# The MLP up product of a one-core encoder block, half of its K-tiles taken as seven quarter products

## The chip, the cores and the metric

The kernel runs on one core of a Trainium2 chip. The metric is the device time of one execution in microseconds, the median of three runs. The engines are named as the profile names them: PE is TensorE (PEld its weight loads), DVE VectorE, ACT ScalarE, POOL GpSimd, SP SyncE, whose queue issues nearly all DMAs here.

## The reference

One layer of an encoder for 256 tokens of width 2,048, all in float32. Only the last product group (the MLP) is touched in its arithmetic:

```python
    for l in range(DEPTH):                       # DEPTH = 1
        xn = rmsnorm(h, norm_mix_w[l])
        proj = xn @ w_in[l]                      # 2,048 x 14,352
        ...                                      # gated linear attention, spatial gating, gates
        h = h + mixed @ w_out[l]
        hn = rmsnorm(h, norm_mlp_w[l])
        h = h + jnp.square(jax.nn.relu(hn @ w_ff_up[l])) @ w_ff_down[l]   # 2,048 x 8,192 and back
    return rmsnorm(h, norm_final_w)
```

## The kernel before, in words

The 256 tokens are two halves (`tt` = 0, 1) of 128. Every large product runs in `gemm`: for one block of 512 output columns it walks the 16 K-tiles of 128 rows in eight pairs. For each pair it loads a 128 x 1,024 block of weights (512 KB, tile `w`), and `split_weights` makes two tiles of it: `wh`, the weights rounded to fp32r (a cast on ACT, line 183), and `wl`, the rest (a subtraction on DVE, line 184). Activations lie transposed as such a pair too (an `Operand`: `hi` and `lo`, in tiles of the pool `slots`, 4 K-tiles each). A product is then three matmuls of 128 x 128 by 128 x 512 into one PSUM bank: hi by `wh`, lo by `wh`, hi by `wl` (lines 201 to 203). So one pair of weight tiles serves 2 K-tiles x 2 halves x 3 = 12 matmuls. There are five `w` buffers and four each of `wh` and `wl`, so ACT casts into a buffer that PE gave back three pieces before the piece is needed.

A finished column block is evicted, and what is to be done with it later (transposes by DVE and a round trip through a DRAM tile `scratch`, in `to_operand_vector`; transposes by PE in `to_operand`) is put on the list `pending`; `gemm` takes one entry off it for each pair of K-tiles (`drain`). Below this code a list scheduler sets each engine's order; semaphores and buffers are set by it too.

The MLP runs in four stages of 2,048 features: `up(st, j)` makes one of the four column blocks of the hidden layer (ACT evicts with relu and the norm's factor, line 353; DVE squares, line 764), and alternates with `down(st - 1, j)`, which multiplies the stage before by its rows of `w_ff_down` and adds the result to `h` on DVE (line 779). PSUM is two pools of four banks: `mm` for the products, `tr` for the rest.

Of the kernel before, what the change touches and what calls it, by code (L numbers as in the profile page):

```python
# [37 lines left out]


W_ROW = 1024  # L40

V_MLP, V_GLA, V_BA, V_BS = 0, 16, 20, 28
NVEC = 36
# [15 lines left out]
def block_kernel(  # L59
# [75 lines left out]
            pending.popleft()()  # L135


    h = cpool.tile([P, NTT, D], F32, name="h")
    xv = x[0].rearrange("(t p) d -> p t d", p=P)

    def load_x(b):
        s = cols(b, 2 * P)
        nc.sync.dma_start(h[:, :, s], xv[:, :, s])

    def late(dst, src):

# [27 lines left out]
    def split_weights(src, by_k=False):  # L174

        k, n = src.shape[1], src.shape[1] * src.shape[2]
        w = wpool.tile([P, W_ROW], F32, tag="w", name=uid("w"), bufs=5)
        hi = wpool.tile([P, W_ROW], F32R, tag="wh", name=uid("wh"), bufs=4)
        lo = wpool.tile([P, W_ROW], F32R, tag="wl", name=uid("wl"), bufs=4)
        wv, hv, lv = [t[:, 0:n].rearrange("p (k n) -> p k n", k=k) for t in (w, hi, lo)]  # L180
        for s in [slice(i, i + 1) for i in range(k)] if by_k else [slice(0, k)]:
            nc.sync.dma_start(wv[:, s], src[:, s])  # L182
            pin(nc.scalar.copy(hv[:, s], wv[:, s]))  # L183
            pin(nc.vector.tensor_tensor(  # L184
                lv[:, s], wv[:, s], hv[:, s].bitcast(F32), op=ALU.subtract
            ))
        return hv, lv

    def gemm(a, w, c0, n=CB, parts=1, k0=0, after=None, split_tail=False):

        ps = [[mm_ps() for _ in range(NTT)] for _ in range(parts)]
        m = n // parts
        held = []

        def products(kt, tt, hi, lo):
            ah, al = a.at(kt, tt)
            for i in range(parts):
                o = ps[i][tt][:, 0:m]
                wh = hi[kt % 2][:, cols(i, m)]
                wl = lo[kt % 2][:, cols(i, m)]  # L200
                pin(nc.tensor.matmul(o, lhsT=ah, rhs=wh, start=kt == 0, stop=False))  # L201
                pin(nc.tensor.matmul(o, lhsT=al, rhs=wh, start=False, stop=False))  # L202
                pin(nc.tensor.matmul(o, lhsT=ah, rhs=wl, start=False, stop=kt == KT - 1))  # L203

        for kb in range(KT // 2):
# [12 lines left out]
            if kb > 1 or kb == 1 and len(pending) > 6:  # L218
                drain()
            while a.ready < 2 * kb + 2:  # L220
                drain()
            if split_tail and kb >= KT // 2 - 3:
# [12 lines left out]
    def to_operand_pair(dst, src, scale=None):  # L235
# [11 lines left out]
        hi, lo = dst.hi[-1], dst.lo[-1]  # L247
        if scale is None:
# [15 lines left out]
        dst.ready += 2  # L264

    def to_operand(dst, src, scale=None):

        for half in range(2):
            part = [src[:, tt, cols(half, 2 * P)] for tt in range(NTT)]
            pending.append(lambda part=part: to_operand_pair(dst, part, scale))  # L270

    def transpose_quadrants(dst, src, jm):

# [2 lines left out]
        for i in range(4):  # L276
            nc.vector.transpose(dv[cols(jm, 32), i], sv[cols(i, 32), jm])  # L277

    def to_operand_vector(dst, src, scale=None):


        tr = []
# [14 lines left out]
        def split():  # L297
            kt0 = dst.ready
            hi, lo = slot(F32R), slot(F32R)
            dst.hi.append(hi)  # L300
            dst.lo.append(lo)

            v = flat(tr[1]).rearrange("p (m a b) -> p a m b", m=4, b=32)

            def by_quadrant(t):
                return t.rearrange("p k (t m b) -> p (k t) m b", t=NTT, b=32)

            if scale is None:
                nc.scalar.copy(by_quadrant(hi), v)  # L309
                nc.vector.tensor_tensor(  # L310
                    by_quadrant(lo), v, by_quadrant(hi).bitcast(F32), op=ALU.subtract
                )
            else:
                for k in range(4):
                    a = slice(NTT * k, NTT * (k + 1))
                    nc.scalar.activation(  # L316
                        by_quadrant(tr[0])[:, a], v[:, a], AF.Copy, scale=scale(kt0 + k)
                    )
                nc.scalar.copy(hi, tr[0])
                nc.vector.tensor_tensor(lo, tr[0], hi.bitcast(F32), op=ALU.subtract)  # L320
            dst.ready += 4

        pending.append(transpose)
# [35 lines left out]
    xsq = [cpool.tile([P, 4], F32, name=f"xsq{tt}") for tt in range(NTT)]  # L359

    def x_step(kb):
        to_operand_pair(xT, [h[:, tt, cols(kb, 2 * P)] for tt in range(NTT)], mix_col)

    def x_next(kb):
        if kb < KT // 2 - 1:
            load_x(kb + 1)
        for i in range(kb - 1, kb + kb // (KT // 2 - 1)):
            if i >= 0:
                b, tt = divmod(i, 2)
                sum_squares(xsq[tt][:, b : b + 1], h[:, tt, cols(b)])  # L370
        if kb < KT // 2 - 1:
            x_step(kb + 1)

# [372 lines left out]


    hT = Operand()
    hsq = [cpool.tile([P, 4], F32, name=f"hsq{tt}") for tt in range(NTT)]
    for j in range(4):  # L750
        ps = gemm(mT, w_out[0], j * CB)[0]
        part = h[:, :, cols(j)]
        for tt in range(NTT):
            nc.vector.tensor_tensor(part[:, tt], ps[tt], part[:, tt], op=ALU.add)
        (to_operand_vector if j < 3 else to_operand)(hT, part, lambda kt: vcol(V_MLP + kt))
# [11 lines left out]
    n_st = D_FF // D  # L767
    fsq = [cpool.tile([P, 4], F32, name=f"fsq{tt}") for tt in range(NTT)]
    wf = []

# [2 lines left out]

    def down(st, j, f):
        last = st == n_st - 1
        ps = gemm(f, w_ff_down[0], j * CB, k0=st * D, split_tail=last and j == 3)[0]
        for tt in range(NTT):
            part = h[:, tt, cols(j)]
# [20 lines left out]
    def finish(tt, m3):  # L799
# [3 lines left out]
        nc.gpsimd.tensor_tensor(r, m, mhalf[:, 0:1], op=ALU.pow)  # L803
        for j in range(4):
            t = ev_tile()
            part = h[:, tt, cols(j)]
            if j == 0:
                nc.vector.tensor_scalar_mul(t, part, r)
            elif j < 3:
# [57 lines left out]
```

## Time and profile before

| | |
|---|---|
| median of three runs | 1631.16 us |
| shortest of them | 1631.15 us |
| the profiled execution's own time | 1629.94 us |
| its span in the profile | 1627.8 us |
| PE busy | 1607.5 us (99%) |
| DVE busy | 958.6 us (59%) |
| ACT busy | 764.7 us (47%) |
| mean DMA rate | 211 GB/s |

The span is the stretch that the profiler saw; the execution's own time is 2.1 us longer, and the median of the runs lies 1.2 us above that. Matmuls are pipelined, so a row of 0.39 us of PE does not mean that PE took 0.39 us for it: how fast it works is read from the starts of rows that follow each other.

### The profile page before, as it was taken

How to read it: one execution, taken by the hardware profiler on the slowest of the kernel's cores; microseconds unless marked ns; L12 is line 12 of the kernel's file. 1: busy time of each engine (PE TensorE's matmuls, PEld its weight loads, DVE VectorE, ACT ScalarE, POOL GpSimd, SP SyncE). 2: the span in 40 equal slices, each digit the busy share in tenths (PEclk: the TensorE clock that was granted, in tenths of full speed). 3: DMA queues.
4: the chain of work that ended last, by engine and by line, in shares of the span. 5: the costliest groups of instructions: out<-in, count | busy, mean ns of one | idle time of the engine just before them, and what ended most of it. 6: DMA issues, size and time to landing. Idle time of an engine off the chain costs nothing.

```text
span 1627.8 us, 19169 instructions
## 1 busy us (share of the span) xinstructions
PE 1607.5 (99%) x7224; PEld 1331.3 (82%) x7224; DVE 958.6 (59%) x1053; ACT 764.7 (47%) x879; POOL 23.3 (1%) x50
## 2 busy tenths in 40 slices
PE   8999999999999999999999999999999999999997
PEld 6877888888888888888888888888888888888886
DVE  5759555555555667766655656555555555555554
ACT  6475455454444444444445544444444444444443
POOL 0000000000000000000000000000000000000000
PEclk9999999999999999999999999999999999999999
DMA  7565666766666767677757777766666666767753
GB/s 242 162 200 170 180 203 202 240 207 200 200 213 184 217 209 213 219 227 225 227 186 242 219 225 241 245 220 219 219 218 213 207 214 214 223 218 220 243 194 113
DMA packets 184821, 343.20 MB, mean 211 GB/s; under 512 B 12340, under 2 KB 31080, under 8 KB 184728
## 3 DMA queue, kind: packets, MB, share of 16 engines
q1 hardware_dynamic: 181744, 337.82, 66.7%
q10 hardware_dynamic: 2984, 4.16, 0.8%
q8 instruction: 56, 0.92, 0.2%
q14 instruction: 37, 0.30, 0.1%
HBM read 324.10 MB, written 17.83 MB: 210 GB/s over the span
## 4 chain that ended last, share of the span: by engine, by line
PE 97%; DVE 1%; issue 0%; ACT 0%; DMA 0%; SPq 0%; POOL 0%; ACTq 0%; POOLq 0%; DVEq 0%
PE mm L201 32%; PE mm L203 32%; PE mm L202 32%; DVE slot L277 1%; PE tr L588 1%; DVE wl L184 1%; PE tr L636 1%; PE tr L731 0%; DMA h<-in_x_dram 0%; PE tr L245 0%; ACT wh L183 0%; PE tr L491 0%; POOL col L333 0%; SPq L182 0%; PE tr L439 0%
## 5 line engine op out<-in xcount | busy, mean ns | idle before, releaser
L184 DVE TENSOR_TENSOR wl<-w,wh 128x1024 fp32r<-128x1024 f32 (+2 forms) x585 | 704.4, 1206 | 611.0 <-ACT wh L183 594.5
L183 ACT CAST wh<-w 128x1024 fp32r<-128x1024 f32 (+2 forms) x585 | 608.0, 1040 | 779.4 <-PE mm L202 758.4
L201 PE MATMUL mm<-wh,slot 128*128 128x512 f32 (+1 forms) x2336 | 905.6, 388 | 2.2 <-ACT pair L468 2.2
L203 PE MATMUL mm<-wl,slot 128*128 128x512 f32 (+1 forms) x2336 | 903.5, 387 | 2.3 <-DVE wl L184 2.3
L202 PE MATMUL mm<-wh,slot 128*128 128x512 f32 (+1 forms) x2336 | 903.1, 387 | 0.0
L203 PEld LDWEIGHTS mm<-wl,slot 128*128 128x128 f32 x2336 | 438.9, 188 | 93.7 <-DVE wl L184 4.5
L201 PEld LDWEIGHTS mm<-wh,slot 128*128 128x128 f32 x2336 | 439.1, 188 | 90.7 <-ACT pair L468 2.4
L202 PEld LDWEIGHTS mm<-wh,slot 128*128 128x128 f32 x2336 | 439.1, 188 | 88.0
L353 ACT ACTIVATE pair<-mm,rstd 128x512 f32<-128x512 f32 x58 | 39.5, 688 | 28.5 <-PE mm L203 28.3
L289 DVE STREAM_TRANSPOSE slot<-pair 128x512 f32<-128x512 f32 x54 | 36.1, 696 | 0.8
L333 POOL TENSOR_TENSOR col<-col,mhalf 128x1 f32<-128x1 f32 (+1 forms) x20 | 17.9, 895 | 863.9 <-DVE col L331 575.8
L310 DVE TENSOR_TENSOR slot<-slot,slot 128x1024 fp32r<-128x1024 f32 x23 | 28.0, 1218 | 2.1 <-ACT slot L309 2.1
L277 DVE STREAM_TRANSPOSE slot<-pair 32x256 f32<-32x256 f32 x64 | 27.9, 436 | 1.0
L779 DVE TENSOR_TENSOR h<-mm,h 128x512 f32<-128x512 f32 x32 | 22.0, 692 | 6.8 <-PE mm L203 6.8
L309 ACT CAST slot<-slot 128x1024 fp32r<-128x1024 f32 x23 | 24.1, 1048 | 0.0
L764 DVE TENSOR_TENSOR pair<-pair 128x1024 f32<-128x1024 f32 x16 | 19.5, 1219 | 0.0
L339 ACT ACTIVATE ev<-h 128x512 f32<-128x512 f32 x24 | 15.0, 626 | 7.9 <-DVE h L779 7.9
L260 DVE SCALAR_TENSOR_TENSOR slot<-tr,mixw,slot 128x256 fp32r<-128x256 f32 x16 | 7.0, 480 | 11.5 <-ACT slot L255 11.5
L316 ACT ACTIVATE slot<-slot,vec 128x256 f32<-128x256 f32 x28 | 11.9, 498 | 0.0
L255 ACT ACTIVATE slot<-tr,mixw 128x256 fp32r<-128x256 f32 x16 | 6.7, 471 | 10.6 <-PE tr L245 10.6
L671 DVE SCALAR_TENSOR_TENSOR pair<-mm,rstd,bg 128x512 f32<-128x512 f32 x16 | 11.4, 750 | 0.0
L718 DVE TENSOR_TENSOR pair<-pair,slot 128x512 f32<-128x512 f32 x16 | 11.0, 685 | 0.1
(103 smaller groups left out, 269.5 us busy)
## 6 DMA issues: line engine op xcount, KB each, us to landing
w<-in_w_in_dram SPq DMA_DIRECT2D x215, 512.0 KB, 3.8
w<-in_w_ff_up_dram SPq DMA_DIRECT2D x128, 512.0 KB, 3.8
w<-in_w_ff_down_dram SPq DMA_DIRECT2D x128, 512.0 KB, 3.5
w<-in_w_branch_dram SPq DMA_DIRECT2D x64, 512.0 KB, 4.1
w<-in_w_out_dram SPq DMA_DIRECT2D x32, 512.0 KB, 4.8
scratch<-slot SPq DMA_DIRECT2D x120, 128.0 KB, 2.7
slot<-scratch SPq DMA_DIRECT2D x30, 512.0 KB, 5.6
w<-in_w_in_dram SPq DMA_DIRECT2D x16, 264.0 KB, 2.7
```

The source lines that it names most:

```text
L183: pin(nc.scalar.copy(hv[:, s], wv[:, s]))
L184: pin(nc.vector.tensor_tensor(lv[:, s], wv[:, s], hv[:, s].bitcast(F32), op=ALU.subtract))
L201: pin(nc.tensor.matmul(o, lhsT=ah, rhs=wh, start=kt == 0, stop=False))
L202: pin(nc.tensor.matmul(o, lhsT=al, rhs=wh, start=False, stop=False))
L203: pin(nc.tensor.matmul(o, lhsT=ah, rhs=wl, start=False, stop=kt == KT - 1))
L277: nc.vector.transpose(dv[cols(jm, 32), i], sv[cols(i, 32), jm])
L289: nc.vector.transpose(blocks[:, tt], sv[:, tt])
L309: nc.scalar.copy(by_quadrant(hi), v)
L310: nc.vector.tensor_tensor(by_quadrant(lo), v, by_quadrant(hi).bitcast(F32), op=ALU.subtract)
L353: nc.scalar.activation(res[:, tt, :], ps[tt], func, scale=scale[tt])
L764: nc.vector.tensor_tensor(a, a, a, op=ALU.mult)
L779: nc.vector.tensor_tensor(part, ps[tt], part, op=ALU.add)
```

## The change

The hidden layer is now made in eight stages of 1,024 features (two column blocks), each made whole before the `down` products of the stage before it. The first stage is still made by `gemm`. While it runs, the entries of `prepare` come off `pending`, two at a time: they scale the transposed activations by the norm's factor (`row_scale`, `norm`), and build the left factors of the scheme, seven quarters or sums and differences of quarters of 128 tokens x 512 of K, each split in hi and lo.

The seven other stages are made by `pair_gemm`. Of the 16 K-tiles, the first 8 go by Strassen's scheme (in Winograd's form): the tokens are halved, the 1,024 rows of K are halved, the 1,024 columns are halved, and in place of eight products of quarters there are seven, named "1" to "7". The right factors are four weight blocks and sums of them, made on DVE in fp32 for two K-tiles at a time: one sum in a tile `s`, three in place in the `w` tiles (`b01`, `b00`, `b10`). A factor is split as before, and serves 6 matmuls (2 K-tiles x 3). The other 8 K-tiles are done plainly (`plain`, 12 matmuls for each split). The seven results lie in all eight PSUM banks together with the plain ones, and are joined by DVE after the last product (lines 939 to 955). One pair of column blocks has thus 7 x 12 + 96 = 180 matmuls, where `gemm` has 192.

Beside this: eight `w` buffers in place of five; `h` lies in four tiles of the pool `slots`, is given up after its norm and loaded again from `x` for the residual; `x` is loaded two blocks ahead; the second part of the one product that is computed in two parts (`parts=2`) has its banks from `tr`; the squares are made on ACT; the `down` products walk 8 K-tiles for each block, so that they are added to `h` twice as often.

```diff
+W_BUFS = 8
...
-    h = cpool.tile([P, NTT, D], F32, name="h")
+    h = [pair_tile() for _ in range(4)]
...
-        w = wpool.tile([P, W_ROW], F32, tag="w", name=uid("w"), bufs=5)
+        w = wpool.tile([P, W_ROW], F32, tag="w", name=uid("w"), bufs=W_BUFS)
...
-    def gemm(a, w, c0, n=CB, parts=1, k0=0, after=None, split_tail=False):
-
-        ps = [[mm_ps() for _ in range(NTT)] for _ in range(parts)]
+    def gemm(a, w, c0, n=CB, parts=1, k0=0, nk=KT, after=None, split_tail=False, jobs=1):
+
+        ps = [[(tr_ps if i else mm_ps)() for _ in range(NTT)] for i in range(parts)]
...
     def x_next(kb):
-        if kb < KT // 2 - 1:
-            load_x(kb + 1)
+        for b in (1, 2) if kb == 0 else (kb + 2,):
+            if b < KT // 2:
+                load_x(b)
...
+    h = []
     for j in range(4):
+        part = pair_tile()
+        h.append(part)
+        late(part, xv[:, :, cols(j)])
         ps = gemm(mT, w_out[0], j * CB)[0]
...
-    def up(st, j, f):
-        ps = gemm(hT, w_ff_up[0], st * D + j * CB)[0]
-        a = scaled(ps, rstd2, AF.Relu)
-        nc.vector.tensor_tensor(a, a, a, op=ALU.mult)
-        to_operand_vector(f, a)
...
+    def row_scale(dst, rstds):
+
+        tp = tr_ps()
+        for tt in range(NTT):
+            wide = ev_tile()[:, 0:P]
+            nc.scalar.activation(wide, ident, AF.Identity, scale=0.0, bias=rstds[tt])
+            nc.tensor.matmul(tp[:, cols(tt, P)], lhsT=wide, rhs=ident, start=True, stop=True)
+        nc.vector.tensor_copy(dst, tp[:, 0:T])
...
+        steps = [lambda: row_scale(row, rstds)]
+        steps += [lambda b=b: norm(b) for b in range(2)]
+        steps.append(lambda: (plain("1", 0, 0), plain("2", 0, 1)))
+        steps.append(lambda: difference("5", 0, (1, 0), (1, 1), sub))
+        steps.append(lambda: difference("6", 1, 0, (0, 0), sub))
+        steps.append(lambda: difference("3", 0, 1, (0, 1), add))
+        steps.append(lambda: difference("7", 1, (0, 0), (1, 0), sub))
+        steps.append(lambda: plain("4", 1, 1))
+        steps += [lambda b=b: (norm(b), rest(b)) for b in (2, 3)]
...
+    def pair_gemm(a, w, c):
+
+        bank = {n: mm_ps() for n in "243N"}
+        bank.update({n: tr_ps() for n in "1567"})
...
+        def product(name, k, src):
+            hi, lo = split(src)
+            ah, al = a.left[name]
+            for kk in range(2):
+                x, y = ah[:, k + kk, :], al[:, k + kk, :]
+                accumulate(
+                    name, ((x, hi[:, kk]), (y, hi[:, kk]), (x, lo[:, kk])),
+                    name in "1567" and k + kk == SK - 1,
+                )
...
+        order = [(kt, block) for kt in range(0, KT - 2 * SK, 2) for block in range(2)]
+        order = order[:5] + [order[6], order[5], order[7]]
+        rest = iter(order)
+        for k in range(0, SK, 2):
+            b00, b10, b11, b01 = (
+                fetch(kh * SK + k, nh) for kh, nh in ((0, 0), (1, 0), (1, 1), (0, 1))
+            )
+            s1 = weights("s", F32, 1)
+            add(s1, b00, b01)
+            add(b01, b01, b11)
+            product("1", k, b00)
+            product("2", k, b10)
+            plain(*next(rest))
+            product("3", k, b11)
+            product("5", k, s1)
+            add(b00, b00, b01)
+            plain(*next(rest))
+            product("7", k, b01)
+            product("6", k, b00)
+            add(b10, b10, b00)
+            if k == 0:
+                plain(*next(rest))
+            product("4", k, b10)
...
+            for a in pair_gemm(hM, w_ff_up[0], (c0, c0 + CB)):
+                nc.scalar.activation(a, a, AF.Relu)
+                nc.scalar.activation(a, a, AF.Square)
+                to_operand_vector(f, a)
...
-    prev = None
-    for st in range(n_st + 1):
-        f = Operand()
+    prev = hidden(0)
+    for st in range(1, n_st + 1):
+        f = hidden(st) if st < n_st else None
...
         for j in range(4):
-            if st < n_st:
-                up(st, j, f)
-            if prev is not None:
-                down(st - 1, j, prev)
+            down(st - 1, j, prev)
```

The scheduler's result can be read from the built programs. PE has 7,008 matmuls of the kind of lines 201 to 203 before and 6,924 after, of which 1,260 are those of the seven pairs. On DVE, in the middle of one `down` block before, nearly every row is a split (line 184), each for 12 matmuls; `slot` is an operand's part and `mm` a PSUM bank:

```order
L184 TENSOR_TENSOR wl_1572_8241<-w_1570_8239,wh_1571_8240 128x1024
L184 TENSOR_TENSOR wl_1577_8263<-w_1575_8261,wh_1576_8262 128x1024
L184 TENSOR_TENSOR wl_1580_8281<-w_1578_8279,wh_1579_8280 128x1024
L310 TENSOR_TENSOR slot_1569_8224<-slot_1554_8142,slot_1568_8223 128x1024
L184 TENSOR_TENSOR wl_1583_8299<-w_1581_8297,wh_1582_8298 128x1024
L779 TENSOR_TENSOR h_78<-mm_1542_8097,h_78 128x512
L779 TENSOR_TENSOR h_78<-mm_1543_8098,h_78 128x512
L184 TENSOR_TENSOR wl_1586_8317<-w_1584_8315,wh_1585_8316 128x1024
```

After, on DVE, in the middle of one pair, from the split for product "6" of the first half (`wl_1793`) to the split for the fourth plain piece (`wl_1810`); `s_1803` is the sum for product "5" of the second half, and `w_1802` its block `b01`:

```order
L871 TENSOR_TENSOR wl_1793_9130<-w_1771_9031,wh_1792_9129 128x1024
L902 TENSOR_TENSOR s_1803_9176<-w_1799_9168,w_1802_9174 128x1024
L871 TENSOR_TENSOR wl_1796_9143<-w_1794_9140,wh_1795_9142 128x1024
L902 TENSOR_TENSOR w_1802_9174<-w_1802_9174,w_1801_9172 128x1024
L871 TENSOR_TENSOR wl_1798_9159<-w_1772_9033,wh_1797_9158 128x1024
L871 TENSOR_TENSOR wl_1805_9180<-w_1799_9168,wh_1804_9179 128x1024
L871 TENSOR_TENSOR wl_1807_9190<-w_1800_9170,wh_1806_9189 128x1024
L902 TENSOR_TENSOR w_1799_9168<-w_1799_9168,w_1802_9174 128x1024
L902 TENSOR_TENSOR w_1800_9170<-w_1800_9170,w_1799_9168 128x1024
L871 TENSOR_TENSOR wl_1810_9202<-w_1808_9199,wh_1809_9201 128x1024
```

Four sums stand between the splits now; the first of them needs the last of the four blocks.

On SP, where the loads are issued in order, one `up` block before stands among the stores and the reload of `scratch` like this:

```order
L182 DMA w_1575_8261<-in_w_ff_up_dram 128x2x512
L294 DMA scratch_1555_8145<-slot_1553_8141 32x4x256 x4
L182 DMA w_1578_8279<-in_w_ff_up_dram 128x2x512
L182 DMA w_1581_8297<-in_w_ff_up_dram 128x2x512
L295 DMA slot_1554_8142<-scratch_1555_8145 128x1024
L182 DMA w_1584_8315<-in_w_ff_up_dram 128x2x512
```

Here each load is for one split. After, the loads for the second half of the same pair (`w_1799` to `w_1802` are its blocks `b00`, `b10`, `b11`, `b01`; `w_1787`, `w_1794` and `w_1808` are plain pieces):

```order
L146 DMA w_1787_9101<-in_w_ff_up_dram 128x2x512
L146 DMA w_1794_9140<-in_w_ff_up_dram 128x2x512
L146 DMA w_1799_9168<-in_w_ff_up_dram 128x2x512
L146 DMA w_1800_9170<-in_w_ff_up_dram 128x2x512
L146 DMA w_1801_9172<-in_w_ff_up_dram 128x2x512
L146 DMA w_1802_9174<-in_w_ff_up_dram 128x2x512
L146 DMA w_1808_9199<-in_w_ff_up_dram 128x2x512
```

The block `b01` is the last of the four; its load waits until DVE has done the split of the second plain piece (`wl_1789`, made of `w_1787`), which gives its buffer back.

## Rows read from the trace of the kernel before

**Rows 1.** The page: span, busy time, granted clock in 40 slices, last chain by engine.

```profile
span 1627.8 us, 19169 instructions
...
PE 1607.5 (99%) x7224; PEld 1331.3 (82%) x7224; DVE 958.6 (59%) x1053; ACT 764.7 (47%) x879; POOL 23.3 (1%) x50
...
PEclk9999999999999999999999999999999999999999
...
PE 97%; DVE 1%; issue 0%; ACT 0%; DMA 0%; SPq 0%; POOL 0%; ACTq 0%; POOLq 0%; DVEq 0%
```

**Rows 2.** Groups by line, 1000 to 1600 us: busy, mean ns | idle before.

```profile
L184 DVE TENSOR_TENSOR wl<-w,wh 128x1024 fp32r<-128x1024 f32 x221 | 270.1, 1223 | 260.1 <-ACT wh L183 249.7 <-DMA w<-in_w_ff_up_dram 10.5
L183 ACT CAST wh<-w 128x1024 fp32r<-128x1024 f32 x221 | 232.9, 1054 | 320.2 <-PE mm L202 316.9 <-PE mm L203 1.9 <-ACT ev L339 1.4
L779 DVE TENSOR_TENSOR h<-mm,h 128x512 f32<-128x512 f32 x30 | 20.6, 692 | 1.5 <-PE mm L203 1.5
...
L310 DVE TENSOR_TENSOR slot<-slot,slot 128x1024 fp32r<-128x1024 f32 x14 | 17.1, 1218 | 0.0
L289 DVE STREAM_TRANSPOSE slot<-pair 128x512 f32<-128x512 f32 x26 | 17.0, 691 | 0.4
L764 DVE TENSOR_TENSOR pair<-pair 128x1024 f32<-128x1024 f32 x13 | 15.8, 1219 | 0.0
```

**Rows 3.** Timeline of PE: start, length; twelve matmuls lie between the line-203 rows.

```profile
1201.97 0.39 PE L203 MATMUL mm<-wl,slot 128*128 128x512 f32 x1
...
1202.20 0.39 PE L201 MATMUL mm<-wh,slot 128*128 128x512 f32 x1
...
1204.69 0.39 PE L203 MATMUL mm<-wl,slot 128*128 128x512 f32 x1
```

**Rows 4.** Waits, whole span: total us, times, longest.

```profile
PEld mm L203 <- DVE wl L184: 4.5, 6, 2.0
...
PE tr L245 <- DMA h<-in_x_dram: 2.7, 1, 2.7
...
PE mm L201 <- ACT pair L468: 2.2, 1, 2.2
```

**Rows 5.** The last chain, 880 to 1000 us: four PE transposes of 128 x 128.

```profile
926.67 0.44 PE tr L245 x4
```

**Rows 6.** Timeline of DVE, 1210 to 1260 us.

```profile
1226.20 1.37 DVE L779 TENSOR_TENSOR h<-mm,h 128x512 f32<-128x512 f32 x2
...
1230.45 1.22 DVE L184 TENSOR_TENSOR wl<-w,wh 128x1024 fp32r<-128x1024 f32 x1 [1.50 <-ACT wh L183]
...
1250.76 1.22 DVE L764 TENSOR_TENSOR pair<-pair 128x1024 f32<-128x1024 f32 x1
1252.01 1.31 DVE L289 STREAM_TRANSPOSE slot<-pair 128x512 f32<-128x512 f32 x2
```

**Rows 7.** Timeline of DVE, 118 to 135 us, where its rows follow each other closely.

```profile
130.34 1.22 DVE L184 TENSOR_TENSOR wl<-w,wh 128x1024 fp32r<-128x1024 f32 x1
131.47 1.22 DVE L556 TENSOR_TENSOR slot<-slot,slot 128x1024 f32<-128x1024 f32 x1
132.61 2.35 DVE L184 TENSOR_TENSOR wl<-w,wh 128x1024 fp32r<-128x1024 f32 x2
```

**Rows 8.** DMA issues, 1000 to 1600 us: KB each, median us from issue to landing.

```profile
w<-in_w_ff_up_dram SPq DMA_DIRECT2D x92, 512.0 KB, 3.8
...
slot<-scratch SPq DMA_DIRECT2D x13, 512.0 KB, 5.6
```

**Rows 9.** The tile `w`, 1000 to 1600 us: landing of all its loads.

```profile
DMA to landing us min/median/max: 3.4/3.7/8.8
```

**Rows 10.** The last chain, 0 to 30 us: the first matmuls, and one later.

```profile
9.04 0.43 PE mm L201
...
12.88 0.40 PE mm L201
...
20.58 0.24 PE mm L201
```

**Rows 11.** Windows: us, busy by engine, granted clock, DMA share, GB/s.

```profile
1100.00:1600.00 500.00, 500.00 (x2208) 414.01 (x2207) 280.54 (x257) 218.47 (x226) 0.00 (x0) 1.00 0.68 217
1600.00:1628.00 28.00, 18.52 (x82) 15.01 (x80) 9.38 (x16) 7.66 (x12) 1.09 (x2) 0.87 0.23 75
```

More of the change, by code (lines that the diff above doesn't have):

```diff
@@ L181, in split_weights @@
         for s in [slice(i, i + 1) for i in range(k)] if by_k else [slice(0, k)]:
-            nc.sync.dma_start(wv[:, s], src[:, s])
+            load(wv[:, s], src[:, s])
             pin(nc.scalar.copy(hv[:, s], wv[:, s]))
@@ L202, in products @@
                 pin(nc.tensor.matmul(o, lhsT=al, rhs=wh, start=False, stop=False))
-                pin(nc.tensor.matmul(o, lhsT=ah, rhs=wl, start=False, stop=kt == KT - 1))
-        for kb in range(KT // 2):
+                pin(nc.tensor.matmul(o, lhsT=ah, rhs=wl, start=False, stop=kt == nk - 1))
+        for kb in range(nk // 2):
             r0 = k0 + kb * 2 * P
@@ L218, in gemm @@
             if kb > 1 or kb == 1 and len(pending) > 6:
-                drain()
+                drain(jobs)
             while a.ready < 2 * kb + 2:
                 drain()
-            if split_tail and kb >= KT // 2 - 3:
+            if split_tail and kb >= nk // 2 - 3:
                 held.append((kb, hi, lo))
@@ L320, in split @@
                 nc.vector.tensor_tensor(lo, tr[0], hi.bitcast(F32), op=ALU.subtract)
+                if keep is not None:
+                    keep.append(tr[0])
             dst.ready += 4
@@ L758, in block_kernel, with __init__ @@
     rstd2 = [row_rstd(hsq[tt], f"rstd2{tt}") for tt in range(NTT)]
-    def up(st, j, f):
-        ps = gemm(hT, w_ff_up[0], st * D + j * CB)[0]
-        a = scaled(ps, rstd2, AF.Relu)
-        nc.vector.tensor_tensor(a, a, a, op=ALU.mult)
-        to_operand_vector(f, a)
-    n_st = D_FF // D
+    SK = 4
+    class Mixed:
+        def __init__(self):
+            self.left = {}
+            self.rest = Operand()
+    def row_scale(dst, rstds):
[5 more added lines that the diff above has]
+        nc.vector.tensor_copy(dst, tp[:, 0:T])
@@ new lines, in normed, with norm, rest, quarter @@
+    def normed(src, rstds):
+        m = Mixed()
+        row = ev_tile()[:, 0:T]
+        def norm(b):
+            nc.vector.tensor_tensor(
+                src[b], src[b], row.unsqueeze(1).broadcast_to([P, 4, T]), op=ALU.mult
+            )
+        def rest(b):
+            hi, lo = slot(F32R), slot(F32R)
+            m.rest.hi.append(hi)
+            m.rest.lo.append(lo)
+            nc.scalar.copy(hi, src[b])
+            nc.vector.tensor_tensor(lo, src[b], hi.bitcast(F32), op=ALU.subtract)
+            m.rest.ready += 4
+        def quarter(i, j):
+            return src[j][:, :, cols(i, P)]
+        room, temp = [], []
+        def split_left(name, v):
+            if not room:
+                room.extend(
+                    tuple(t.rearrange("p k (s t) -> p s k t", s=2)[:, i] for t in pair)
+                    for pair in [(slot(F32R), slot(F32R))] for i in range(2)
+                )
+            hi, lo = room.pop(0)
+            nc.scalar.copy(hi, v)
+            nc.vector.tensor_tensor(lo, v, hi.bitcast(F32), op=ALU.subtract)
+            m.left[name] = hi, lo
+        def plain(name, i, j):
+            split_left(name, quarter(i, j))
+        def difference(name, i, a, b, op):
+            if not temp:
+                t = slot().rearrange("p k (s t) -> p s k t", s=2)
+                temp.extend(t[:, k] for k in range(2))
+            get = lambda v: temp[v] if isinstance(v, int) else quarter(*v)
+            nc.vector.tensor_tensor(temp[i], get(a), get(b), op=op)
+            split_left(name, temp[i])
+        sub, add = ALU.subtract, ALU.add
+        steps = [lambda: row_scale(row, rstds)]
[7 more added lines that the diff above has]
+        steps += [lambda b=b: (norm(b), rest(b)) for b in (2, 3)]
+        return m, steps
@@ new lines, in weights, with split, accumulate, fetch @@
+    def weights(tag, dt, bufs):
+        t = wpool.tile([P, W_ROW], dt, tag=tag, name=uid(tag), bufs=bufs)
+        return t.rearrange("p (k n) -> p k n", k=2)
+    def pair_gemm(a, w, c):
+        bank = {n: mm_ps() for n in "243N"}
+        bank.update({n: tr_ps() for n in "1567"})
+        begun = set()
+        def split(src):
+            hi, lo = weights("wh", F32R, 4), weights("wl", F32R, 4)
+            nc.scalar.copy(hi, src)
+            nc.vector.tensor_tensor(lo, src, hi.bitcast(F32), op=ALU.subtract)
+            return hi, lo
+        def accumulate(name, terms, last):
+            for n, (x, y) in enumerate(terms):
+                nc.tensor.matmul(
+                    bank[name], lhsT=x, rhs=y, start=name not in begun,
+                    stop=last and n == len(terms) - 1,
+                )
+                begun.add(name)
+        def product(name, k, src):
+            hi, lo = split(src)
+            ah, al = a.left[name]
+            for kk in range(2):
+                x, y = ah[:, k + kk, :], al[:, k + kk, :]
+                accumulate(
+                    name, ((x, hi[:, kk]), (y, hi[:, kk]), (x, lo[:, kk])),
+                    name in "1567" and k + kk == SK - 1,
+                )
+        def fetch(row, block):
+            t = weights("w", F32, W_BUFS)
+            load(
+                t, w[row * P : (row + 2) * P, c[block] : c[block] + CB].rearrange(
+                    "(k p) n -> p k n", p=P
+                ),
+            )
+            return t
+        def add(dst, x, y):
+            nc.vector.tensor_tensor(dst, x, y, op=ALU.add)
+        def plain(kt0, block):
+            hi, lo = split(fetch(2 * SK + kt0, block))
+            drain()
+            for kk in range(2):
+                for tt in range(NTT):
+                    x, y = a.rest.at(kt0 + kk, tt)
+                    accumulate(
+                        ("24", "3N")[block][tt], ((x, hi[:, kk]), (y, hi[:, kk]), (x, lo[:, kk])),
+                        kt0 + kk == KT - 2 * SK - 1,
+                    )
+        order = [(kt, block) for kt in range(0, KT - 2 * SK, 2) for block in range(2)]
[4 more added lines that the diff above has]
+                fetch(kh * SK + k, nh) for kh, nh in ((0, 0), (1, 0), (1, 1), (0, 1))
+            )
+            s1 = weights("s", F32, 1)
[11 more added lines that the diff above has]
+            add(b10, b10, b00)
+            if k == 0:
+                plain(*next(rest))
+            product("4", k, b10)
+        p1, u2, u3, v, z = (ev_tile() for _ in range(5))
+        nc.scalar.copy(p1, bank["1"])
+        add(u2, bank["6"], p1)
+        add(u3, bank["7"], u2)
+        nc.vector.tensor_tensor(v, bank["5"], u2, op=ALU.subtract)
+        nc.vector.tensor_tensor(z, bank["5"], u3, op=ALU.subtract)
+        res = [pair_tile() for _ in range(2)]
+        left = list(rest)
+        for n, (kt, block) in enumerate(left):
+            plain(kt, block)
+            if all(b != block for _, b in left[n + 1 :]):
+                for tt in range(NTT):
+                    add(
+                        res[block][:, tt, :], bank[("24", "3N")[block][tt]],
+                        ((p1, u3), (v, z))[block][tt],
+                    )
+        return res
@@ new lines, in block_kernel, with hidden @@
+    FK = 8
+    hM, prepare = normed(scaled_h, rstd2)
+    def hidden(st):
+        f = Operand()
+        c0 = st * 2 * CB
+        if st == 0:
+            pending.extend(prepare)
+            for j in range(2):
+                a = scaled(gemm(hT, w_ff_up[0], c0 + j * CB, jobs=2)[0], rstd2, AF.Relu)
+                nc.scalar.activation(a, a, AF.Square)
+                to_operand_vector(f, a)
+        else:
+            for a in pair_gemm(hM, w_ff_up[0], (c0, c0 + CB)):
+                nc.scalar.activation(a, a, AF.Relu)
+                nc.scalar.activation(a, a, AF.Square)
+                to_operand_vector(f, a)
+        return f
@@ L775, in down @@
         last = st == n_st - 1
-        ps = gemm(f, w_ff_down[0], j * CB, k0=st * D, split_tail=last and j == 3)[0]
+        ps = gemm(
+            f, w_ff_down[0], j * CB, k0=st * FK * P, nk=FK, split_tail=last and j == 3
+        )[0]
         for tt in range(NTT):
-            part = h[:, tt, cols(j)]
+            part = h[j][:, tt, :]
             nc.vector.tensor_tensor(part, ps[tt], part, op=ALU.add)
@@ L805, in finish @@
             t = ev_tile()
-            part = h[:, tt, cols(j)]
+            part = h[j][:, tt, :]
             if j == 0:
```

28 lines of the change are left out of this document (18 added, 10 removed).

## The prediction

> **What bounds the kernel now.** I read the page first: PE is busy 99% of the span at the full granted clock, and 97% of the last chain is its own work [rows 1]. In the MLP it is the same: over 500 us PE is never idle, while DVE works 280.5 us of them and ACT 218.5 [rows 11]. The groups by line say why the other two idle: ACT's casts wait for PE to give a weight buffer back (316.9 us) and DVE's splits wait for those casts [rows 2]. So the time is the number of matmuls times their spacing. The spacing is read from starts: twelve matmuls take 2.72 us, 0.2267 each [rows 3].
>
> **The matmuls removed.** Seven pairs of column blocks lose 192 - 180 = 12 each, 84 in all, as the count of the built programs says too (7,008 to 6,924). 84 x 0.2267 = 19.04 us, all of it on the bounding engine. This is 1.2% of the time, and no other term of the change removes PE work.
>
> **A wait removed.** The product in two parts takes all four `mm` banks, and the next product waits for ACT's evictions: PE stands 2.2 us at line 468 [rows 4]. Its second part now lies in `tr`, so the next product finds two free banks: -2.2 us. What is late next there is nothing that the rows show.
>
> **Matmuls added.** `row_scale` has two small ones. The nearest row is the PE transposes, 0.44 us for four [rows 5]: 0.2 us. They stand in PE's queue behind the norm's factor (a chain through DVE, POOL and ACT which PE did not wait for before); they come off `pending` in the second pair of K-tiles or later, some 5 us after the last `w_out` block. I take no wait, and 1 us as the upper end.
>
> **The preparation.** While the first stage runs, DVE gets 4 scalings of 128 x 1,024 (1.22), 7 splits and 4 sums of 128 x 512 (0.69, the nearest row is line 779) and 2 large splits (1.22), with the copy of the row some 15.3 us [rows 2]. Taken two at a time they fall on about 5.5 pairs of K-tiles, 15 us of PE. In each DVE idles 1.50 us as it is [rows 6], 8.2 us. The 7.1 us too many are first paid from the lead: a buffer comes back three pieces (8.16 us) before its next use, of which cast and split need 1.05 + 1.22, so 5.9 us. The rest stalls PE: +1.2 us. Ends: 0, if some steps fall into the second column block, and 7.1 without the lead.
>
> **The seven pairs.** DVE is the engine to look at. Added work: 6 more splits (1.223), 8 sums (1.219) and 8 joining adds (0.692) for each pair, 8 more adds for each stage's `down` blocks less the squares that go to ACT. One stage of PE is (180 + 192) x 0.2267 = 84.3 us; DVE has 38 splits, 8 sums, 16 adds, 4 transposes and 2 operand splits in it: 46.5 + 9.8 + 11.1 + 2.8 + 2.4 = 72.6 us, 86%. ACT has 38 casts of 1.05, with two relus, two squares and the rest under 50. So neither binds on average; but the work lies unevenly. A product's split now feeds 6 matmuls (1.36 us), and sums stand between splits.
>
> I walked one pair, with t = 0 at its first matmul. PE's pieces without stalls: "1" 0, "2" 1.36, plain 2.72, "3" 5.44, "5" 6.80, plain 8.16, "7" 10.88, "6" 12.24, plain 13.60, "4" 16.32; second half: "1" 17.68, "2" 19.04, plain 20.40. DVE's rows that follow each other start 1.14 us apart although each is 1.22 long [rows 7]; one that needs the row before it starts 1.25 later [rows 6]. DVE finishes the third piece's split at about 0.5, adds the last `down` block to `h` (1.37 for two [rows 6]) until 1.8, and splits for "3", "5" and the second plain piece by 5.3. That last one frees the buffer into which the fourth block of the second half, `b01`, is loaded. A load lands 3.8 us after its issue [rows 8]: 9.1. DVE meanwhile splits for "7" and "6"; the buffer for "6" comes back at 6.80, its cast ends at 7.85, the split at 9.1. From there nine rows stand in DVE's order up to the split of the plain piece due at 20.40: sum, split, sum, three splits, sum, sum, split. They start at 9.1, 10.2, 11.4, 12.5, 13.7, 14.8, 15.9, 17.2, 18.3, and the last ends at 19.6. PE needs it at its third matmul, 20.40 + 0.45 = 20.85. So the tightest place has 1.3 us to spare; behind it no sum is left, and pace is set again by ACT's wait for buffers. The joining adds run beside the three last plain pieces (8.2 us), and their banks are needed by the first `down` block only after these.
>
> Thus a stall appears when `b01` lands more than 5.1 us after its issue. The loads of `w` land in 3.4 to 8.8 us, median 3.7 [rows 9]; here they are issued some 2 us apart. I take 0.3 us for each pair on average, 7 x 0.3 = +2.1. Ends: 0, and 7 x 3.7 = 26 if each took the longest.
>
> At this place a rule of the skill speaks against the change. Rows 7 show that a DVE row starts before the one ahead has ended. The Trainium skill's "VectorE: DVE Perf Modes", section Terms, says that each operation is followed by a drain and that the next can't issue until the pipe is empty; read as full lengths, 1.25 for each row, the walk would end at 20.8 and leave nothing to spare. The rows decide for 1.14, but the rule is why the first rival has a chance of a quarter.
>
> **Other edits.** The loads are the same number of bytes but for 2 MB of `x` again, beside an average DMA share of 0.68 [rows 11]; they are issued from ACT's queue ahead of the `w_out` blocks, under its waits for PE [rows 2]. Cost 0; if a load waited for a buffer of `slots`, ACT's casts behind it would wait, and the 5.9 us lead covers that. Eight `w` buffers and `x` two blocks ahead: at the start PE waits 2.7 us for `x` and 4.5 us for splits [rows 4]. The splits wait behind transposes on DVE, not for loads, so I take 0, and -7.2 as the lower end.
>
> **Sum.** Against the execution's own 1629.94: -19.04 - 2.2 + 0.2 + 1.2 + 2.1 = -17.7, 1612.2. The median lies 1.2 above that execution: **1613.4 us**, 1.1% faster.
>
> **Rivals.** *DVE is late in each pair* by about 1 us at the fourth plain piece (slower rows, own waits, or landings of some 6 us). For it: the spare time is only 1.3 us out of a walk of twenty rows. Against: the 1.14 of rows 7. It gives 7 x 1.0 in place of 2.1: 1618; with 2 us, 1625.
>
> *The load of `b01` is late and the change loses*: DVE works in order, so the sum that lacks `b01` holds the splits of five pieces that already have their data. Without this term the gain is 19.8 us, 2.8 for each pair; it is gone when the load takes 3.8 + 1.3 + 2.8 = 7.9 us. At 9 us each pair loses 3.9: 1631.2 - 19.8 + 27.3 = 1639. For it: 8.8 occurs [rows 9], and the reloads of `scratch` take 5.6 [rows 8]. Against: the median.
>
> *The clock falls.* At the start ten matmuls run at 0.43 in place of 0.23 until the clock is up from its lower level of 1.2 GHz to 2.4 GHz (9.04 to 12.88) [rows 10], 2 us; the granted clock falls to 0.87 of full in the last window, where PE is busy two thirds of the time [rows 11]. If short stalls in each half of a pair did this, 14 x 2 = 28: 1641. The Trainium skill's "TensorE: Matmul & The Clock Gate", section A second HAM failure mode: psum-queue depth-cycling, describes a kernel whose clock swings because it goes from bank to bank; a pair goes through eight banks. Against it: this kernel changes banks every three matmuls already, and its clock is full in every slice [rows 1].
>
> *More is gained than the count*: the waits at the start go too, 1613.4 - 7.2 = 1606. That the matmuls aren't fewer is ruled out by the built program.
>
> **Chances.** Forecast (1608 to 1617) 0.57; DVE late (1617 to 1625) 0.24; late load 0.08; clock 0.03; more gained 0.08. From 1607 to 1625 lies some 0.84 of that, with part of the last case. Two per cent, about what a measurement of this kernel can tell from no change, is 32.6 us: the three gains together (19.0 + 2.2 + 7.2 = 28.4) don't reach it, so faster by that 0.01; slower by it needs 7.5 us lost in each pair, 0.03; within it 0.96.
>
> **What would show it.** In the trace after: twelve matmuls still 2.72 us apart in the pairs; 1,260 rows at line 876; no wait at line 468's place; PE's waits for DVE near 0 to 0.5 us in each pair, at the plain piece behind "2" of the second half; DVE about 70% of the span (958.6 + 176) with no gap longer than 1.5 us ahead of the sum for "5"; the page's clock full. Wrong would be the forecast if DVE's splits took longer beside the additional loads, if loads in pairs landed much later than before, or if PE stood at the start of the pairs for a bank.

## The result, and the profile after

The changed kernel takes **1608.14 us** (median of four runs, 1607.76 to 1608.66). The ratio to the kernel before is 0.986, 95% interval 0.984 to 0.988, so 23 us are gained (20 to 26). One of the four runs of the kernel before took 4,878.55 us; the ratio goes by the other three, 1630.40 to 1631.16. The forecast was 1613.4, with 1607 to 1625 as its range and 0.96 for a change within 2%. The profiled execution took 1607.84 us, 22.1 less than that of before; its span is 21.7 shorter.

The page, against [rows 1]:

```profile
span 1606.1 us, 19384 instructions
...
PE 1587.8 (99%) x7144; PEld 1316.0 (82%) x7144; DVE 1112.1 (69%) x1241; ACT 831.5 (52%) x945; POOL 24.2 (2%) x50
...
PEclk9999999999999999999999999999999999999999
...
PE 95%; DVE 2%; issue 0%; ACT 0%; ACTq 0%; POOLq 0%; DVEq 0%
```

PE still fills 99% of the span, at the full granted clock. DVE, which the scheme loads most, rose from 959 to 1112 us.

Whether the pairs stall is read from where each begins. The last chain, from 955 us (start, length; "x6" are the six matmuls of product "1"):

```profile
963.46 1.36 PE tr L876 x6
...
1047.78 1.36 PE tr L876 x6
...
1132.10 1.36 PE tr L876 x6
...
1469.38 1.36 PE tr L876 x6
```

From one stage to the next pass 84.32 us each time, and (180 + 192) matmuls x 0.22667 are 84.32: PE waits for nothing in any of the seven stages. The list of PE's waits is empty from 963 to 1590 us.

The timeline of DVE in the pair that begins at 1132.10 shows how near that was, against the walk:

```profile
1138.43 2.58 DVE L871 TENSOR_TENSOR wl<-w,wh 128x1024 fp32r<-128x1024 f32 x2 [1.29 <-ACT wh L870]
1140.95 1.23 DVE L902 TENSOR_TENSOR s<-w,w 128x1024 f32<-128x1024 f32 x1
1142.10 1.22 DVE L871 TENSOR_TENSOR wl<-w,wh 128x1024 fp32r<-128x1024 f32 x1
1143.23 1.22 DVE L902 TENSOR_TENSOR w<-w,w 128x1024 f32<-128x1024 f32 x1
1144.37 3.49 DVE L871 TENSOR_TENSOR wl<-w,wh 128x1024 fp32r<-128x1024 f32 x3
1147.77 2.48 DVE L902 TENSOR_TENSOR w<-w,w 128x1024 f32<-128x1024 f32 x2
1150.17 2.36 DVE L871 TENSOR_TENSOR wl<-w,wh 128x1024 fp32r<-128x1024 f32 x2
```

PE's timeline has the pair's first matmul and the first one that uses the split for the fourth plain piece (the chain counts a matmul from the end of the one ahead, 0.17 later, hence 1132.10 there):

```profile
1131.93 0.62 PE L876 MATMUL tr<-wh,slot 128*128 128x512 f32 x2
...
1152.79 0.39 PE L876 MATMUL mm<-wl,slot 128*128 128x512 f32 x1
```

The sum for "5" starts 9.02 after the pair's begin (the walk had 9.1); the split for the fourth plain piece starts at 1150.17 and ends 1.22 later, at 19.46 (walk: 19.6). So 1.40 us were to spare (the expectations below have 1.56 or 1.6, counted from the chain's begin), and 1.27 to 1.42 in every pair but the first. DVE's idle time ahead of the sum is for a cast of ACT, but the block `b01` came hardly earlier: it landed 3.66 us after its issue, 0.12 before the sum. From the second pair on it landed 3.6 to 3.8 us after its issue and the sum followed 0.1 behind. In the first pair DVE's order is another, the sum starts at 14.45, and the least spare is 0.97, at the last plain piece. The rows start 1.13 to 1.14 apart where they don't need each other, as in [rows 7].

By stretches, before 963 us, the times differ in four places. At the start, this row of PE's timeline of the kernel before

```profile
47.46 0.72 PE L203 MATMUL mm<-wl,slot 128*128 128x512 f32 x2 [1.54 <-DVE wl L184]
```

stands 1.5 us earlier after:

```profile
45.96 0.72 PE L206 MATMUL mm<-wl,slot 128*128 128x512 f32 x2 [1.55 <-DVE wl L187]
...
942.31 0.73 PE L206 MATMUL mm<-wl,slot 128*128 128x512 f32 x2 [1.00 <-DVE wl L187]
```

The wait of [rows 4] at line 468 is gone, 2.5 us from the next common point. The second of the two rows above is the preparation's stall, 1.0 us; `row_scale` stands in the chain a little ahead of it:

```profile
924.51 0.46 PE tr L797 x4
```

So for the last matmul, 21.3 us earlier: -1.5 - 2.5 + 0.5 + 1.0 - 19.04 = -21.5, with 0.2 in small gaps. The tail behind it is 0.4 shorter.

Loads did change. The landing of all loads of `w` from 1000 to 1600 us, against [rows 9]:

```profile
DMA to landing us min/median/max: 3.6/4.9/8.6
```

The median is 1.2 us longer, at the same mean DMA share (0.68 from 1100 to 1600 us, as in [rows 11]). But it is the loads of `w_ff_down` that land later, not those of the pairs. The issues of that stretch (KB each, median us to landing), first those of `w_ff_down` before, then both after; `w_ff_up` before is in [rows 8], 3.8:

```profile
w<-in_w_ff_down_dram SPq DMA_DIRECT2D x128, 512.0 KB, 3.5
...
w<-in_w_ff_down_dram SPq DMA_DIRECT2D x121, 512.0 KB, 5.4
w<-in_w_ff_up_dram SPq DMA_DIRECT2D x96, 512.0 KB, 3.9
```

No product was late by it. Two groups of DVE by line, 1000 to 1600 us, against [rows 2]:

```profile
L187 DVE TENSOR_TENSOR wl<-w,wh 128x1024 fp32r<-128x1024 f32 x128 | 155.4, 1221 | 90.4 <-ACT wh L186 88.7 <-DMA scratch<-slot 1.5 <-DMA w<-in_w_ff_down_dram 0.2
L871 DVE TENSOR_TENSOR wl<-w,wh 128x1024 fp32r<-128x1024 f32 x121 | 146.3, 1221 | 27.5 <-ACT wh L870 24.2
```

A split takes the 1.22 us that it took before, and DVE's idle time is still the wait for ACT's casts. Of it 24.2 us are left in the pairs (line 871) and 88.7 in the `down` blocks, from 249.7 before: the room was unevenly used. The other signs that the prediction named are there too: line 876 has 616 + 308 + 224 + 112 = 1,260 matmuls in the page, and DVE is at 69%. Its rows' full lengths add up to 175.8 us more than before, the prediction's 176; the page counts time in which rows overlap once, hence 153.5.

### The profile page after: what moved, and what is told of

It is laid out like the page before. It is cut to its first block, busy times and chain, and to the rows that moved or that the text cites. A ratio compares the mean times of both kernels' runs of the same rounds, so it can differ in the third digit from the quotient of the medians.

```text
span 1606.1 us, 19384 instructions
## 1 busy us (share of the span) xinstructions
PE 1587.8 (99%) x7144; PEld 1316.0 (82%) x7144; DVE 1112.1 (69%) x1241; ACT 831.5 (52%) x945; POOL 24.2 (2%) x50
## 4 chain that ended last, share of the span: by engine, by line
PE 95%; DVE 2%; issue 0%; ACT 0%; ACTq 0%; POOLq 0%; DVEq 0%
PE mm L206 25%; PE mm L204 25%; PE mm L205 25%; PE mm L876 13%; PE tr L876 5%; PE tr L602 1%; PE tr L650 1%; DVE wl L187 0%; PE tr L745 0%; DVE slot L806 0%; DVE slot L287 0%; DVE slot L831 0%; PE tr L205 0%; PE tr L204 0%; PE tr L206 0%
## 5 line engine op out<-in xcount | busy, mean ns | idle before, releaser
L187 DVE TENSOR_TENSOR wl<-w,wh 128x1024 fp32r<-128x1024 f32 (+2 forms) x473 | 566.3, 1202 | 406.8 <-ACT wh L186 398.7
L186 ACT CAST wh<-w 128x1024 fp32r<-128x1024 f32 (+2 forms) x473 | 489.1, 1035 | 585.4 <-PE mm L205 517.9
L206 PE MATMUL mm<-wl,slot 128*128 128x512 f32 (+1 forms) x1856 | 720.0, 388 | 3.4 <-DVE wl L187 3.3
L204 PE MATMUL mm<-wh,slot 128*128 128x512 f32 (+1 forms) x1856 | 722.1, 389 | 0.0
L205 PE MATMUL mm<-wh,slot 128*128 128x512 f32 (+1 forms) x1856 | 720.0, 388 | 0.0
L204 PEld LDWEIGHTS mm<-wh,slot 128*128 128x128 f32 x1856 | 349.0, 188 | 70.8
L205 PEld LDWEIGHTS mm<-wh,slot 128*128 128x128 f32 x1856 | 349.0, 188 | 70.1
L870 ACT CAST wh<-w 128x1024 fp32r<-128x1024 f32 x140 | 147.5, 1055 | 116.9 <-PE mm L876 62.9
L871 DVE TENSOR_TENSOR wl<-w,wh 128x1024 fp32r<-128x1024 f32 x140 | 169.3, 1221 | 32.9 <-ACT wh L870 29.2
L876 PE MATMUL mm<-wh,slot 128*128 128x512 f32 x616 | 189.7, 389 | 0.0
L876 PEld LDWEIGHTS mm<-wh,slot 128*128 128x128 f32 x616 | 115.7, 188 | 23.9
L876 PE MATMUL mm<-wl,slot 128*128 128x512 f32 x308 | 119.9, 389 | 0.0
L876 PE MATMUL tr<-wh,slot 128*128 128x512 f32 x224 | 69.0, 389 | 0.0
```

The costliest lines, as they stand in the source:

```text
L187: pin(nc.vector.tensor_tensor(lv[:, s], wv[:, s], hv[:, s].bitcast(F32), op=ALU.subtract))
L870: nc.scalar.copy(hi, src)
L871: nc.vector.tensor_tensor(lo, src, hi.bitcast(F32), op=ALU.subtract)
L876: nc.tensor.matmul(bank[name], lhsT=x, rhs=y, start=name not in begun, stop=last and n == len(terms) - 1,)
```

## The experiments

**The stages made plainly again.** All stages use `gemm`; the seven products, the preparation and `row_scale` go, everything else of the change stays.

```diff
-            for a in pair_gemm(hM, w_ff_up[0], (c0, c0 + CB)):
-                nc.scalar.activation(a, a, AF.Relu)
+        for j in range(2):
+            a = scaled(gemm(hT, w_ff_up[0], c0 + j * CB)[0], rstd2, AF.Relu)
```

> All stages' up products made plainly, with everything else of the change kept (eight w buffers, x two blocks ahead, banks from tr, stages of 1,024 features, squares on ACT). The preparation and row_scale go too. Main theory (the saving in the stages is the 84 matmuls, the pairs stall nowhere): 84 x 0.2267 = 19.0 us come back, the preparation's stall of 1.0 and row_scale's 0.8 go: 1608.1 + 19.0 - 1.8 = 1625.3 (1624 to 1627), so still about 5 to 6 us faster than before. Rival (the gain lies in the other edits, the pairs give back what their matmuls save): 1612 or less.

Measured: 1625.49 us, ratio to before 0.997 (0.996 to 0.998). PE's waits in this kernel (us in total, times, longest) hold nothing behind the first ones:

```profile
PE tr L170 <- DMA ev<-in_norm_mix_w_dram: 3.5, 1, 3.5
PE mm L206 <- DVE wl L187: 2.3, 4, 1.5
PE tr L248 <- DMA pair<-in_x_dram: 2.0, 1, 2.0
```

The main theory holds: the stages are worth 17.35 net, where 19.04 - 1.0 - 0.5 = 17.5 were counted, and some 5 us (3 to 7 by the interval) come from the rest. In the traces of this kernel and the one before they are 4.2: 2.5 the wait at line 468, 0.4 behind the last matmul, and 1.3 at the start, which the experiment on `x` below shows to be mostly scatter. Between the two the matmuls keep their distance, so the other edits gain and cost nothing there.

**One wait alone.** The kernel before with only this:

```diff
-        ps = [[mm_ps() for _ in range(NTT)] for _ in range(parts)]
+        ps = [[(tr_ps if i else mm_ps)() for _ in range(NTT)] for i in range(parts)]
```

> The kernel before with one edit of the change alone: the second part of the product in two parts has its banks from tr. Main theory (the wait at line 468 is for banks alone and nothing takes its place): 1631.2 - 2.2 to 2.5 = 1628.7 to 1629.0. Rival (another wait takes its place): 1631.

Measured: 1627.0 us, ratio 0.998 (0.997 to 0.999), 2 to 5 us faster. The wait at line 468 isn't in the list of PE's waits any more, and nothing stands in its place:

```profile
PE tr L167 <- DMA ev<-in_norm_mix_w_dram: 3.4, 1, 3.4
PE tr L245 <- DMA h<-in_x_dram: 3.1, 1, 3.1
PE mm L203 <- DVE wl L184: 2.3, 4, 1.5
```

The profiled span is 2.2 shorter than before. The median is 1.7 lower than the lowest expected; that counted from 1631.2, and beside this run the kernel before took 1630.39. The edit is worth its wait and is independent of the scheme.

**x one block ahead.** Lookahead as before the change:

```diff
-        for b in (1, 2) if kb == 0 else (kb + 2,):
-            if b < KT // 2:
-                load_x(b)
+        if kb < KT // 2 - 1:
+            load_x(kb + 1)
```

> x is loaded one block ahead, as before the change; everything else as changed. If the 1.5 us that PE's first 46 us became shorter are from loading x two blocks ahead: 1609.6, and the matmul that stood at 45.96 stands at 47.5 again. If they are from the weight buffers or the order of the queue: 1608.1, and it stays at 46.0.

Measured: 1608.21 us, and the matmul stands at 46.34: the lookahead is worth nothing that can be seen. Nor is it fixed that the start is 1.5 us shorter. In the seven other profiled executions with the change's start that matmul stands between 45.91 and 47.20, in the two with the old one at 47.35 and 47.46; five buffers in place of eight gave the 45.91, and the 47.20 has the same code there as the 45.96. Two things differ between the ten executions: PE waits 1.5 to 3.4 us for the first block of `x`, and 3 to 10 of the distances between the first matmuls' starts are 0.43 us and not 0.23, as in [rows 10] (9 in the execution before, 3 in the one after, which is 1.0 of the 1.5). Much of the 1.5 is thus the spread of one execution against another. Whether some tenths belong to the change stays open.

**Fewer weight buffers.**

```diff
-W_BUFS = 8
+W_BUFS = 5
```

> Five w buffers in place of eight in the changed kernel. Main theory (the pair stands on the lead of the loads: four blocks must lie in SBUF together, and three plain pieces beside them): with five buffers the loads of b11 and b01 wait for products that are only just made, and PE waits in each pair for the sums, 2 to 4 us: 1608 + 7 x (2 to 4) = 1622 to 1637, the waits at lines 871 and 876 of the stages. Rival (the loads' lead is not needed, ACT's wait for wh sets the pace): 1608 to 1610.

Measured: 1629.73 us, ratio to before 0.9995 (0.9985 to 1.0005): the whole gain is gone. The last chain through one pair that begins at 1140.00:

```profile
1149.94 2.37 DVE wl L871 x2
...
1152.33 4.96 DMA w<-in_w_ff_up_dram
...
1157.31 1.24 DVE s L902
...
1158.57 1.24 DVE w L902
...
1160.98 1.23 DVE wl L871
...
1162.22 4.88 DMA w<-in_w_ff_up_dram
...
1167.20 1.05 ACT wh L870
...
1168.30 1.20 PE mm L876 x4
```

A split gives a buffer back, `b01` is loaded into it, the sum for "5" waits for the landing (17.5 us after the pair's first matmul, where eight buffers had 9.02), and a split further on frees the buffer of the next load. Two landings or three, 4.9 us each here and 3.7 to 6.2 in the other pairs, now stand in the chain of each pair. Pairs begin 86.7 to 87.2 us apart in place of 84.3, and the first one costs 5.5 more: 5.5 + 6 x 2.7 = 21.7, against 21.6 measured. The rival of the prediction that let the load of `b01` be late was a real mechanism; eight buffers keep it away. Its price was too high, though: by the walk a sum that starts 8.5 us later, with 1.40 to spare, would cost 7.1. With five buffers the scheduler placed the other splits ahead of the sum, so they weren't held behind it.

The same with `W_BUFS = 7`:

> Seven w buffers in place of eight in the changed kernel. The tightest split has 1.56 us to spare with eight. A buffer fewer brings the load of b01 behind a split that comes one piece later in the row, 1.1 to 2.7 us. Main theory: 0 to 0.5 us late in each pair, 1608 to 1612. Rival (the eighth buffer carries the scheme): 2 us or more in each pair, 1622.

Measured: 1610.58 us, ratio to before 0.988 (0.987 to 0.989). Its one wait of PE in the stages is in the first pair:

```profile
PE mm L876 <- ACT wh L870: 0.3, 1, 0.3
```

That pair is 0.9 us longer, the others not at all, though their spare at the fourth plain piece fell to 1.01 to 1.25. The profiled execution (1609.99) is 2.15 above that of eight buffers; the other 1.2 lie in its start (47.19 against 45.96), within the scatter seen above. So the main theory holds, but for one pair in place of each.

**More work on DVE in each pair.** The sum for "5" of the second half is made again, with the same value each time.

```diff
             s1 = weights("s", F32, 1)
-            add(s1, b00, b01)
+            for _ in range(1 + (3 if k else 0)):
+                add(s1, b00, b01)
```

> The sum for product 5 of each pair's second half is made four times in place of once (the same value each time), 3 x 1.14 to 1.25 = 3.4 to 3.8 us more of DVE in each pair, at or behind the place with 1.6 us to spare. Main theory (DVE's order in the half pair, not its share of the span, is what limits): the scheduler puts the repeats between splits and moves the other sums later, so by counting rows the splits for PE still come in time or late by under 0.6 us: 1608 to 1612. Rival A (the spare is 1.6 us and all three repeats stand ahead of the tight split): 7 x (3.6 - 1.6) = +14, 1622. Rival B (DVE is busy 69%, so there is room): 1608.

Measured: 1611.74 us. The last chain shows who pays:

```profile
1053.55 1.36 PE tr L876 x6
...
1137.87 1.36 PE tr L876 x6
...
1222.18 1.36 PE tr L876 x6
```

From the second pair on the spacing is 84.32: 3.4 us more of DVE in each of them cost next to nothing up to the sixth, and 0.2 in the last. The first pair alone is 3.2 us longer. In it DVE has two transposes and a split of the operand `f` of the first stage more (lines 299 and 320), 2.5 us that later stages do beside their `down` blocks; that these are the reason is argued, no run takes them away. So the number of the main theory was met, but not by its even split over the pairs. Rival A, which took the 1.6 us for all the room there is, falls: the scheduler moved the other sums behind splits, so that one row more stands ahead of the split for the fourth plain piece, whose spare fell to 0.29 in the second pair.

With six more in place of three:

> The same sum made seven times, 6 x 1.14 to 1.25 = 6.8 to 7.5 us more of DVE in each pair; DVE is then busy some 73% of the span. Main theory: the splits at the half's start come 2 to 3 us late in each pair, 1608 + 7 x (2 to 3) = 1622 to 1629, with PE's waits at DVE's wl of line 871 in the pairs alone. Rival B (DVE's share of the span tells what room there is): 1608.

Measured: 1637.59 us, 29.5 more than the changed kernel and slower than before, at DVE 71% busy. Pairs begin 87.8 to 88.1 apart, 3.7 late each, and the first costs 7.6: 7.6 + 6 x 3.7 = 29.8. The direction was expected, the size not (2 to 3 for each pair). The place was wrong too. DVE's timeline in the pair that begins at 1143.41 has a sum at every second row, the last one here:

```profile
1163.72 1.22 DVE L902 TENSOR_TENSOR s<-w,w 128x1024 f32<-128x1024 f32 x1
1164.86 1.22 DVE L871 TENSOR_TENSOR wl<-w,wh 128x1024 fp32r<-128x1024 f32 x1
1165.99 1.22 DVE L902 TENSOR_TENSOR s<-w,w 128x1024 f32<-128x1024 f32 x1
```

and ACT's timeline has

```profile
1167.30 1.05 ACT L870 CAST wh<-s 128x1024 fp32r<-128x1024 f32 x1 [4.22 <-DVE s L902]
```

What is late first is not a split but the cast of the sum; behind it in ACT's order stand the casts for "7" and "6". The list of PE's waits has both, the casts with the larger part:

```profile
PE tr L876 <- ACT wh L870: 7.0, 7, 3.8
PE mm L876 <- ACT wh L870: 3.2, 16, 0.2
PE mm L876 <- DVE wl L871: 2.5, 7, 0.4
```

DVE at 70% cost 3.6 us and at 71% 29.5 us: rival B, that its share of the span tells the room, is refuted.

**The preparation, spread out.** Its steps come one at a time in the first column block, two in the second.

```diff
-                a = scaled(gemm(hT, w_ff_up[0], c0 + j * CB, jobs=2)[0], rstd2, AF.Relu)
+                a = scaled(gemm(hT, w_ff_up[0], c0 + j * CB, jobs=1 + j)[0], rstd2, AF.Relu)
```

> The preparation's steps come off the list one at a time in the first column block of the first stage and two at a time in the second, in place of two throughout. Main theory (the 1.0 us stall there is DVE's work being denser than its idle time and the lead cover): spread over more pairs of K-tiles the stall goes, -1.0 us, 1607.1. Rival (the stall has another cause, the norm's factor or row_scale ahead of it): unchanged, 1608.1.

Measured: **1606.97 us**, the fastest of all (1606.34 to 1607.80, where the changed kernel had 1607.76 to 1608.66); ratio to before 0.986 (0.984 to 0.987). The two ranges touch, and the kernel before took 1630.39 beside this one and 1631.16 beside the changed one, so what tells the two apart is the trace: of five waits for DVE's splits four are left, 2.3 us in place of 3.3, and between 900 and 966 us there is none.

```profile
PE tr L170 <- DMA ev<-in_norm_mix_w_dram: 3.3, 1, 3.3
PE tr L248 <- DMA pair<-in_x_dram: 2.8, 2, 2.7
PE mm L206 <- DVE wl L187: 2.3, 4, 1.5
```

From the late matmul of the start (47.20 here, 45.96 in the changed kernel) to the first pair pass 916.2 us in place of 917.5. The stall came from the density of DVE's work, as the prediction had it.

## Why the prediction was right, and what it mis-sized

- **The matmuls removed, -19.04.** Right: the pairs' spacing is the count times 0.22667, and the plain stages brought 17.35 of 17.5 back.
- **The wait at line 468, -2.2.** Right, 2.5 in the trace of the change; alone 2.2 in the span.
- **row_scale, +0.2.** Mis-sized: 0.45. The two matmuls are four records, so each took what two PE transposes take. No wait for the norm's factor appeared.
- **The preparation, +1.2.** Right: 1.0, and gone where the steps lie further apart.
- **The seven pairs, +2.1.** The largest term that was off among those of the change: 0. The walk's times were good to 0.2 us; the term was an allowance for late landings of `b01`, put at 0.3 for each pair with no row that gives it. None was late: from the second pair on the block landed 3.6 to 3.8 us after its issue, as the walk took it, where the limit was 5.1. The landings that became longer are those of `w_ff_down`. The rivals that make DVE or a load late did not occur, and are real: with five buffers and with six more sums the gain is lost.
- **The start, 0, with -7.2 as its lower end.** 1.5 shorter in this execution, not shown to be the change's.
- **From the execution to the median, +1.2.** 0.3 after. It was scatter too: in the two later measurements the kernel before had medians of 1629.90 and 1630.39, beside the 1629.94 of its profiled execution.

Together these are the 5.3 us by which the forecast was high: 2.1 for the pairs, 1.5 for the start, 0.9 for the median, and 0.8 for the tail, what lies outside the span and the small terms. The start and the median, 2.4 us, are mostly chance and no step of the prediction: they brought the time to the lower edge of its first case (1608 to 1617), which holds 1608.14 by only 0.14. Why the tail is shorter (9.2 us against 9.7 from the last matmul's start) stays open.

One count of the prediction is worded wrongly: its "8 more adds for each stage's `down` blocks" are 4 for a stage of 1,024 features (8 for one of before), and its 176 us are worked out with the right number.

A rule was weighed at the pairs: the Trainium skill's "VectorE: DVE Perf Modes", section Terms, lets no operation issue before the pipe is empty. By that reading nine rows of 1.25 from 9.1 end at 20.35, not at the prediction's 20.8, so 0.5 us would have been left. The runs speak against it where an operation does not use the result of the one ahead: rows of 1.22 us start 1.14 apart. The same page of the Trainium skill, section "Two Vector instructions with no wait between them", agrees with the trace: there only an instruction that is held, for one by a start in another group of partitions, waits for all earlier ones. The clock was the other fear. It stays full in every slice although each pair goes through eight PSUM banks, so that what the Trainium skill's "TensorE: Matmul & The Clock Gate", section A second HAM failure mode: psum-queue depth-cycling, reports of another kernel, where PE idles for moments between groups of matmuls, does not occur here.

## What to carry to other kernels

Fewer matmuls pay their full count only while the engine that prepares their operands stays ahead at its tightest place; walk one period in its order of instructions, since its share of the span says little (69%, 70% and 71% cost 0, 3.6 and 29.5 us here). A scheme that needs several blocks at once needs the buffers to load them early: the same arithmetic with five weight buffers gained nothing. Look at the first period by itself, because work left over from the phase ahead falls into it.

## What was not expected of the hardware

A matmul of 128 x 128 by 128 x 128 in plain float32 (`row_scale`) appears as two records and takes about 0.23 us, as long as one of fp32r with four times the columns (0.2267).

The loads of `w_ff_down` landed 1.9 us later in the median (5.4 against 3.5) at the same mean DMA share of 0.68, without a product waiting for one, while those of `w_ff_up` did not (3.9 against 3.8). Neither the seven products nor the number of buffers is the whole reason: with the stages made plainly the two medians are 4.9 and 3.8, with five buffers 5.6 and 4.0. What these kernels share is that a stage's four `down` blocks stand in a row, where they alternated with `up` blocks before; that this makes the loads land later is not shown, since no run here takes it back alone.
